# Side work of a block's mixers ordered behind the main work on VectorE, and one mixer's norm moved a round later

## The chip, the cores and the metric

The kernel runs on one core of a Trainium2 chip. The metric is the device time of one execution in microseconds (us); three executions of the kernel before were timed, and a further one was profiled.

## What is computed

Two transformer layers (attention and a convolutional MLP, 1024 tokens of width 1024) are followed by one block with four parallel mixers. The change lies in that last block alone. Cut to what matters:

```
proj = h @ w_in                         # 11 slots of 512 columns
(va, za, bb, bc, bv, zb, ca, cg, zc, dv, zd) = split(proj, 11)
ya = rglru(va)                          # a: two-way gated linear scan
yb = bb * depthwise_conv(bc * bv, 3)    # b
u = ca * sigmoid(cg)                    # c: 31-tap depthwise convolution,
u = depthwise_conv(u, c_conv, 15, 15)   #    layer norm over the 512 channels,
u = layer_norm(u, c_ln_g, c_ln_b)       #    silu, 512 x 512 matmul
yc = silu(u) @ c_pw + c_pw_b
yd = (pool_grid(dv) @ d_w + d_b) * d_scale   # d: box means of four sizes
cat = [ya * silu(za), yb * silu(zb), yc * silu(zc), yd * silu(zd)]
x = x + gate * (cat @ w_out);  return rms_norm(x)
```

## The kernel before

Tokens lie along the free axis (1024, as two halves of 512), channels on the 128 partitions. Every fp32 matmul is three fp32r matmuls of high and low pieces (`mm3`): the high piece is cast on ScalarE (ACT, L239), the low one subtracted on GpSimd or VectorE (POOL or DVE, L240). A projected "slot" (one of the 11 column groups, one of four 128-channel chunks c) is 48 matmuls of 128x512 into a two-bank PSUM tile with tag A, of which there are two.

The last block (`block2`) runs four rounds, c = 0 to 3, one 128-channel chunk of every mixer in each. A round emits: `a_conv` (slot 0, copied to SBUF by ACT on L1474, then six taps on DVE, L1327), `d_pool` (slot 9, copied on L1474; two scans on DVE, L1621 and L1625, with windows and products on POOL between and behind them), `mixer_b` (slots 3, 4, 2, 5: products on DVE on L1568 and L1573, a gate on L1493), `a_gates`, `d_end`, then `a_back` (ACT's exponentials after a switch to the table set LNEXP, DVE's products and scans on L1351 to L1354, POOL's sum on L1601), the gate of slot 1, the product for the concatenation (`cat`, L1498), and `out_proj`: the output projection of the chunks that are done, added up by DVE on L1522.

Mixer c is spread over the rounds. `mixer_c(k)` forms the gated input of chunk k (L1557) and puts 30 taps of its convolution (L1549) into a queue of side work, `bg`; each tap is a DVE pass over 1024 tokens. `tick()`, called some twenty times a round, emits the next 2 (from the end of round 0 on, 3) steps of that queue into the program. When the convolutions are through, the queue goes on with `c_var`: per half, mean over the channels (L1647 and L1649 on DVE, a matmul with ones on L1651), subtraction (L1662), squares, mean again. The rest of the norm is `c_norm` (ACT L1675, L1676; three small DVE passes L1677 to L1679; four products L1682, two on DVE and two on POOL, per half), then `c_silu` (ACT L1692, L1693; DVE L1694; the split), and at the end `c_end`, the 512 x 512 matmul with its DVE pass on L1708.

In the kernel before, `bg.drain()` and `c_norm` stand in round 2, `c_norm` behind `a_back`; `c_silu` stands in round 3, ahead of the switch to LNEXP. What comes behind the rounds is `c_end` for both halves, `out_proj` of a's last chunk, and per half the output projection of mixer c and `finish` (scaling, residual, RMS norm; its reciprocal root is Ln and Exp on ACT, L254 and L255).

The emitted order is not the order on the engines: the framework runs a scheduler that lays out each engine's instructions by its own timing model, under the data dependencies and under ordering hints that the kernel adds. A DVE tap of the side queue that is emitted behind a main instruction may so be laid ahead of it. Buffers come from rings: `p` has 5 buffers, `cb` 3, `q` 10.

Of the kernel before, what the change touches and what calls it, by code (L numbers as in the profile page):

```python
# [61 lines left out]
LNEXP, SIG, GELU = "natural_log_exp_and_others", "sigmoid_and_others", "gelu_apprx_tanh_and_others"  # L62
# [33 lines left out]
class Net:  # L96
# [146 lines left out]
    def halves(self, tag):  # L243

        while True:
            t = self.t(tag)
            for k in range(0, BUFS[tag][0], 512):
                yield t[:, k:k + 512]
# [1191 lines left out]
    def block2(self, xs, src):  # L1440
        nc, I = self.nc, self.I
# [2 lines left out]

        rate = [BGN]

        def tick():
            for _ in range(rate[0]):
                bg.step()

        def slots_first():

            load = lambda ss: [self.weight(I["wi2"][s * 4]) for s in ss]
            a = [self.ps("A") for _ in range(2)]
            b = [[], []]
            for n, w in enumerate(load((7, 6))):
                self.proj(w, xs, 0, a[n][:, 0:512])
            ws = load((3, 4))
            for hf, tags in enumerate(("OT", "JT")):
                for n in range(2):  # L1460
                    b[n].append(self.ps(tags[n]))
                    self.proj(ws[n], xs, hf, b[n][hf])
            for n, w in enumerate(load((7, 6))):
                self.proj(w, xs, 1, a[n][:, 512:1024])
            return {(7, 0): a[0], (6, 0): a[1], (3, 0): b[0], (4, 0): b[1]}
# [85 lines left out]
        def mixer_c(c):  # L1551
            pg = slot(7, c)
            t = self.t("q")
            nc.scalar.activation(t, pg, AF.Sigmoid)
            tick()
            pa = slot(6, c)
            nc.vector.tensor_tensor(out=t, in0=pa, in1=t, op=ALU.mult)  # L1557
            y = self.t("v")
            bg.add(conv(y, t, [self.pcol("c_conv", k * 4 + c) for k in range(31)], 15))
            tick()  # L1560
            return y

        def mixer_b(c):
            t = copied("p", slot(3, c))
            tick()
            pv = slot(4, c)
            for o, i in zip(halves(t), pv) if isinstance(pv, list) else ((t, pv),):
                nc.vector.tensor_tensor(out=o, in0=i, in1=o, op=ALU.mult)  # L1568
            tick()
            y = self.t("p")  # L1570
            run(conv(y, t, [self.pcol("b_conv", k * 4 + c) for k in range(3)], 1))
            pb = slot(2, c)
            nc.vector.tensor_tensor(out=y, in0=pb, in1=y, op=ALU.mult)  # L1573
            tick()
            return cat(y, gated(5, c))

        def a_conv(c):
            v = copied("p", slot(0, c))
            tick()
            xs_ = []  # L1580
            for d in range(2):
                xc, xh, xl = self.t("q"), self.t("q", F32R), self.t("q", F32R)
                self.rg_conv(v, T, c, d, xc, (xh, xl))
                xs_.append((xc, (xh, xl)))
            return xs_

        def a_gates(c, xs_):
            gates = self.weight(I["wrg"][c], 512)
            units = []
            for d, (xc, xhl) in enumerate(xs_):  # L1590
                r, th = self.t("q"), self.t("q")
                self.rg_gates(T, c, d, gates, xc, r, th, xhl, self.t("p"))
                units.append((c, d, xc, r, th))
                tick()
            return units
# [18 lines left out]
        def d_pool(c):  # L1614
            ps = slot(9, c)
            u, P, S, mask = copied("p", ps), *(self.t("p") for _ in range(3))
            h = 2 ** c
            ones = lambda n, v: nc.gpsimd.memset(mask.rearrange("p (r q) -> p r q", q=n)[:, :, 0:1], v)
            nc.gpsimd.memset(mask, 1.0)
            ones(64, 0.0)  # L1620
            nc.vector.tensor_tensor_scan(out=P, data0=mask, data1=u, initial=0.0, op0=ALU.mult, op1=ALU.add)  # L1621
            tick()
            window(S.rearrange("p (q r) -> p r q", r=16), P.rearrange("p (r q) -> p r q", q=64), h)
            ones(16, 0.0)
            nc.vector.tensor_tensor_scan(out=P, data0=mask, data1=S, initial=0.0, op0=ALU.mult, op1=ALU.add)  # L1625
            window(S.rearrange("p (r q) -> p q r", q=64), P.rearrange("p (q r) -> p q r", r=16), h)
            rc = self.t("p")
            nc.sync.dma_start(rc, I["rcnt"][c])
            nc.gpsimd.tensor_tensor(out=S, in0=S, in1=rc, op=ALU.mult)
            nc.gpsimd.tensor_tensor(out=S, in0=S, in1=u, op=ALU.subtract)  # L1630
            h, l = self.t("q", F32R), self.t("q", F32R)
            self.split(S, h, l, nc.gpsimd)
            return h, l

        def d_end(c, hl):
            z = gated(10, c)
            wd = self.weight(I["dw"], 512)
            y = self.t("p")
            for hf in range(2):
                ps = self.psM()  # L1640
                self.mm3(ps, [(tuple(p[:, c * 128:c * 128 + 128] for p in wd), tuple(halves(p)[hf] for p in hl))])
                nc.scalar.activation(halves(y)[hf], ps, AF.Identity, scale=self.pcol("d_scale", c), bias=self.dbs[:, c:c + 1])
            return cat(y, z)
# [28 lines left out]
        def c_norm(u, vs):  # L1672
            for hf, var in enumerate(vs):
                a, b = halves(self.t("p"))
                nc.scalar.activation(a, var, AF.Ln, bias=self.lneps, scale=1.0)  # L1675
                nc.scalar.activation(b, a, AF.Exp, scale=-0.5)  # L1676
                nc.vector.scalar_tensor_tensor(out=a, in0=var, scalar=LN_EPS, in1=b, op0=ALU.add, op1=ALU.mult)  # L1677
                nc.vector.scalar_tensor_tensor(out=a, in0=a, scalar=-0.5, in1=b, op0=ALU.mult, op1=ALU.mult)
                nc.vector.scalar_tensor_tensor(out=b, in0=a, scalar=1.5, in1=b, op0=ALU.add, op1=ALU.mult)  # L1679
                for c, p in enumerate(u):  # L1680
                    x = halves(p)[hf]
                    (nc.gpsimd if c % 2 else nc.vector).tensor_tensor(out=x, in0=x, in1=b, op=ALU.mult)  # L1682

        def c_silu(u, hf):

            out = []
            for c, p in enumerate(u):
                t = halves(p)[hf]
                g, bb = self.pcol("ln_g", c), self.pcol("ln_b", c)
                h, l = self.t("x", F32R), self.t("x", F32R)  # L1690
                q = self.t("cb")[:, 0:512]
                nc.scalar.activation(q, t, AF.Sigmoid, scale=g, bias=bb)  # L1692
                nc.scalar.activation(t, t, AF.Identity, scale=g, bias=bb)  # L1693
                nc.vector.tensor_tensor(out=t, in0=t, in1=q, op=ALU.mult)  # L1694
                self.split(t, h, l, nc.gpsimd if c % 2 else nc.vector)
                out.append((h, l))
            return out
# [18 lines left out]
        us, vs = [mixer_c(0)], []  # L1716
# [3 lines left out]
        for c in range(4):  # L1720
            if c:
                ax = a_conv(c)
                dx = d_pool(c)
                catb = mixer_b(c)
            units = a_gates(c, ax)
            catd = d_end(c, dx)
            if c == 3:
                za = gated(1, c)
                z = [gated(8, k) for k in range(4)]
                s = [c_silu(us, hf) for hf in range(2)]  # L1730
            if c == 2:
                bg.drain()
            self.act_set(LNEXP)
            ya = a_back(units)
            if c == 2:
                c_norm(us, vs)
            if c < 3:
                self.act_set(SIG)
                za = gated(1, c)
                for k in ((1, 2), (3,), ())[c]:  # L1740
                    us.append(mixer_c(k))
                    if k == 3:
                        bg.add(c_var(us, vs))
                rate[0] = 3
            if c < 2:
                out_proj([(1, c, catb), (3, c, catd), (0, c, cat(ya, za))], first=c == 0)
            else:
                out_proj([(1, c, catb), (3, c, catd)])
                cata = cat(ya, za)
                if c == 2:  # L1750
                    out_proj([(0, c, cata)])
# [215 lines left out]
```

## Time and profile before

| | |
|---|---|
| time, median of 3 runs | 3844.7 us (3842.88 to 3845.17) |
| profiled execution: time, span | 3847.31 us, 3845.5 us |
| TensorE (PE) busy | 3491.9 us, 91% |
| VectorE, ScalarE, GpSimd busy | 2513.1, 1831.1, 1991.7 us |
| mean granted TensorE clock | 0.969 of full speed |

The span is the time from the first to the last instruction in the profile; the profiled execution's own time is 1.8 us longer and 2.6 us over the median. The last block takes roughly the last 780 us of the span.

### The profile page before, as it was taken

How to read it: one execution, taken by the hardware profiler on the slowest of the kernel's cores; microseconds unless marked ns; L12 is line 12 of the kernel's file. 1: busy time of each engine (PE TensorE's matmuls, PEld its weight loads, DVE VectorE, ACT ScalarE, POOL GpSimd, SP SyncE). 2: the span in 40 equal slices, each digit the busy share in tenths (PEclk: the TensorE clock that was granted, in tenths of full speed). 3: DMA queues.
4: the chain of work that ended last, by engine and by line, in shares of the span. 5: the costliest groups of instructions: out<-in, count | busy, mean ns of one | idle time of the engine just before them, and what ended most of it. 6: DMA issues, size and time to landing. Idle time of an engine off the chain costs nothing. (4 is left out here: it accounts for less than half of the span.)

```text
span 3845.5 us, 47528 instructions
## 1 busy us (share of the span) xinstructions
PE 3491.9 (91%) x16588; PEld 2827.6 (74%) x16588; DVE 2513.1 (65%) x3432; ACT 1831.1 (48%) x3300; POOL 1991.7 (52%) x1480
## 2 busy tenths in 40 slices
PE   6999899889999999999889889999988979898998
PEld 4788678667777777778678767887766768686776
DVE  5566865888888551567885776665545288685547
ACT  4455755444445343355664454545575333324333
POOL 3445433636667564534533546666655454545544
PEclk9999999899999999999999899999989989999999
DMA  3643553432323552454473432222634211111114
GB/s 100 163 119 127 193 170 129 134 123 100 110 88 128 189 173 73 112 135 140 140 231 122 133 116 90 73 82 88 191 120 141 68 45 52 44 50 38 56 50 145
DMA packets 217473, 440.12 MB, mean 114 GB/s; under 512 B 28432, under 2 KB 52240, under 8 KB 217232
## 3 DMA queue, kind: packets, MB, share of 16 engines
q1 hardware_dynamic: 217232, 437.08, 35.5%
q8 instruction: 130, 2.13, 0.2%
q14 instruction: 111, 0.91, 0.1%
HBM read 313.75 MB, written 104.34 MB: 109 GB/s over the span
## 5 line engine op out<-in xcount | busy, mean ns | idle before, releaser
L233 PE MATMUL AZ<-xZ,whZ 128*128 128x512 f32 x2880 | 907.4, 396 | 51.5 <-ACT pZ L1474 14.4
L240 POOL TENSOR_TENSOR wlZ<-wrZ,whZ 128x512 fp32r<-128x512 f32 x340 | 488.7, 1452 | 553.9 <-ACT whZ L239 474.9
L233 PEld LDWEIGHTS AZ<-xZ,whZ 128*128 128x128 f32 x2880 | 545.4, 191 | 178.9 <-issue 20.0
L233 PE MATMUL AZ<-xZ,wlZ 128*128 128x512 f32 x1440 | 567.1, 396 | 10.9 <-POOL wlZ L240 10.7
L524 POOL TENSOR_TENSOR ptZ<-pfZ,ptZ 128x512 fp32r<-128x512 f32 (+1 forms) x200 | 264.2, 1321 | 363.7 <-DVE ptZ L523 337.7
L233 PE MATMUL JZ<-xZ,whZ 128*128 128x512 f32 (+1 forms) x1248 | 403.7, 401 | 41.3 <-ACT whZ L239 21.6
L239 ACT CAST whZ<-wrZ 128x512 fp32r<-128x512 f32 x340 | 196.9, 608 | 431.7 <-issue 141.2
L240 POOL TENSOR_TENSOR wlZ<-qZ,whZ 128x512 fp32r<-128x512 f32 x200 | 279.5, 1413 | 202.7 <-ACT whZ L239 202.7
L233 PEld LDWEIGHTS AZ<-xZ,wlZ 128*128 128x128 f32 x1440 | 275.0, 191 | 74.4 <-POOL wlZ L240 16.8
L522 ACT COPY pfZ<-TZ 128x512 f32<-128x512 f32 (+2 forms) x400 | 220.6, 556 | 211.6 <-PE TZ L517 130.6
L233 PEld LDWEIGHTS JZ<-xZ,whZ 128*128 128x128 f32 (+1 forms) x1248 | 223.1, 186 | 101.0 <-ACT whZ L239 31.5
L540 PE MATMUL OZ<-ptZ,vZ 128*128 128x256 f32 (+1 forms) x1344 | 262.3, 307 | 33.2 <-POOL ptZ L524 12.5
L523 DVE CAST ptZ<-pfZ 128x512 fp32r<-128x512 f32 (+2 forms) x400 | 220.0, 552 | 107.1 <-ACT pfZ L522 91.9
L517 PE MATMUL TZ<-ident,pZ 128*128 128x128 f32 x1488 | 243.7, 284 | 21.6 <-ACT pfZ L522 12.3
L240 POOL TENSOR_TENSOR wlZ<-vZ,whZ 128x512 fp32r<-128x512 f32 x144 | 181.8, 1283 | 149.3 <-ACT whZ L239 149.0
L540 PEld LDWEIGHTS OZ<-ptZ,vZ 128*128 128x128 f32 x1344 | 205.2, 197 | 58.8 <-POOL ptZ L524 16.6
L233 PE MATMUL JZ<-xZ,wlZ 128*128 128x512 f32 (+1 forms) x624 | 245.9, 394 | 0.0
L233 PE MATMUL TZ<-xZ,whZ 128*128 128x512 f32 x736 | 230.2, 394 | 2.6 <-DVE pZ L256 1.5
L517 PEld LDWEIGHTS TZ<-ident,pZ 128*128 128x128 f32 x1488 | 182.0, 145 | 53.6 <-ACT pfZ L522 21.3
L233 PE MATMUL AZ<-qZ,whZ 128*128 128x512 f32 x592 | 191.7, 406 | 31.7 <-ACT pjZ L1157 23.0
L562 DVE TENSOR_REDUCE s1Z<-AZ 128x1 f32<-128x1024 f32 x128 | 156.0, 1221 | 67.1 <-PE AZ L233 35.8
L1549 DVE SCALAR_TENSOR_TENSOR vZ<-qZ,pv,vZ 128x1009 f32<-128x1009 f32 (+14 forms) x120 | 194.8, 1642 | 4.1 <-ACT vZ L1539 2.4
(515 smaller groups left out, 7942.5 us busy)
## 6 DMA issues: line engine op xcount, KB each, us to landing
qZ<-wup SPq DMA_DIRECT2D x80, 512.0 KB, 3.3
wrZ<-wi SPq DMA_DIRECT2D x156, 256.0 KB, 2.7
vZ<-wdn SPq DMA_DIRECT2D x48, 512.0 KB, 3.6
sc_g<-vZ SPq DMA_DIRECT2D x44, 512.0 KB, 3.6
qZ<-sc_pr SPq DMA_DIRECT2D x40, 512.0 KB, 4.9
wrZ<-wo SPq DMA_DIRECT2D x64, 256.0 KB, 2.8
sc_ot<-cbZ SPq DMA_DIRECT2D x56, 256.0 KB, 2.5
xZ<-sc_ot SPq DMA_DIRECT2D x56, 256.0 KB, 5.5
```

Of the source, the lines that this page charges most:

```text
L233: self.nc.tensor.matmul(ps, lhsT=a, rhs=b, start=first and k == 0, stop=last and k == n - 1, skip_group_check=parts)
L239: nc.scalar.copy(h, full)
L240: (eng or nc.vector).tensor_tensor(out=l, in0=full, in1=h.bitcast(F32), op=ALU.subtract)
L517: nc.tensor.transpose(ps[:, n:n + 128], blk, self.ident)
L522: nc.scalar.copy(pf[:, 0:n], ps[:, 0:n])
L523: nc.vector.tensor_copy(ph[:, 0:n], pf[:, 0:n])
L524: (nc.gpsimd if SHARE[self.turn2 % len(SHARE)] else nc.vector).tensor_tensor(out=pl[:, 0:n], in0=pf[:, 0:n], in1=ph[:, 0:n].bitcast(F32), ...
L540: nc.tensor.matmul(o[:, c0:c0 + w], lhsT=v, rhs=x[:, at[k]:at[k] + w], start=(k == order[0] and x is ph), stop=(k == order[-1] and x is pl ...
L562: nc.vector.tensor_reduce(out=nmx, in_=ps, axis=AX.X, op=ALU.max, negate=True)
L1549: nc.vector.scalar_tensor_tensor(out=o, in0=i, scalar=w[k], in1=o, op0=ALU.mult, op1=ALU.add)
```

## The change

It does two things. First, `tick()` now looks at the program emitted since its last call, notes the last DVE instruction of the main work, and gives every DVE instruction of the side steps that it emits a hint to be scheduled behind that one (an order without a semaphore). Second, `bg.drain()` and `c_norm` go from round 2 to round 3; there `c_norm` follows `a_back`, and `c_silu` follows `c_norm` behind one more switch of the table set, back to SIG.

```
+        seen = [0, None]
+        later = mybir.DependencyInfo(mybir.DependencyClass.NoSync, mybir.DependencyReason.SCHED_ONLY)
         def tick():
+            ins = list(nc.cur_bb.bb.instructions)
+            for i in ins[seen[0]:]:
+                if i.engine == mybir.EngineType.DVE:
+                    seen[1] = i.name
+            n = len(ins)
             for _ in range(rate[0]):
                 bg.step()
+            ins = list(nc.cur_bb.bb.instructions)
+            for i in ins[n:]:
+                if seen[1] and i.engine == mybir.EngineType.DVE:
+                    self.tc.add_manual_dep(i, seen[1], later, reason="side")
+            seen[0] = len(ins)
...
             if c == 3:
                 za = gated(1, c)
                 z = [gated(8, k) for k in range(4)]
-                s = [c_silu(us, hf) for hf in range(2)]
-            if c == 2:
                 bg.drain()
             self.act_set(LNEXP)
             ya = a_back(units)
-            if c == 2:
+            if c == 3:
                 c_norm(us, vs)
+                self.act_set(SIG)
+                s = [c_silu(us, hf) for hf in range(2)]
```

The line numbers of the changed kernel are 14 higher inside the block (L1549 becomes L1563, L1573 becomes L1587, L1498 becomes L1512). The order of the instructions on the engines moves as follows.

VectorE, round 0, mixer b. Before: its first products (L1568), its two taps (on tile pZ_27790), the product with slot 2 (L1573) and the gate of slot 5 (L1493); vZ_27614 is the side convolution of chunk 0.

```order
L1568 TENSOR_TENSOR pZ_27781<-TZ_27518,pZ_27781 128x512
L1549 SCALAR_TENSOR_TENSOR vZ_27614<-qZ_27611,pv,vZ_27614 128x1020
L1549 SCALAR_TENSOR_TENSOR vZ_27614<-qZ_27611,pv,vZ_27614 128x1019
L1549 SCALAR_TENSOR_TENSOR pZ_27790<-pZ_27781,pv,pZ_27790 128x1023
L1549 SCALAR_TENSOR_TENSOR vZ_27614<-qZ_27611,pv,vZ_27614 128x1018
L1549 SCALAR_TENSOR_TENSOR pZ_27790<-pZ_27781,pv,pZ_27790 128x1023
L1549 SCALAR_TENSOR_TENSOR vZ_27614<-qZ_27611,pv,vZ_27614 128x1017
L1573 TENSOR_TENSOR pZ_27790<-AZ_27804,pZ_27790 128x1024
```

The same place in the changed kernel:

```order
L1582 TENSOR_TENSOR pZ_27781<-TZ_27518,pZ_27781 128x512
L1563 SCALAR_TENSOR_TENSOR vZ_27614<-qZ_27611,pv,vZ_27614 128x1016
L1563 SCALAR_TENSOR_TENSOR vZ_27614<-qZ_27611,pv,vZ_27614 128x1017
L1563 SCALAR_TENSOR_TENSOR pZ_27790<-pZ_27781,pv,pZ_27790 128x1023 x2
L1587 TENSOR_TENSOR pZ_27790<-AZ_27804,pZ_27790 128x1024
L1563 SCALAR_TENSOR_TENSOR vZ_27614<-qZ_27611,pv,vZ_27614 128x1018
L1563 SCALAR_TENSOR_TENSOR vZ_27614<-qZ_27611,pv,vZ_27614 128x1019
L1507 TENSOR_TENSOR pZ_27915<-AZ_27866,pZ_27915 128x1024
```

From the start of the round to the product with slot 2, 22 side taps stand on VectorE before and 9 in the changed kernel; the other 13 have moved behind it.

VectorE, round 1, mixer a's six taps (tiles qZ_28720 and qZ_28729) and the first scan of mixer d (L1635). In the changed kernel they stand in a row:

```order
L1563 SCALAR_TENSOR_TENSOR vZ_27614<-qZ_27611,pv,vZ_27614 128x1009
L1327 SCALAR_TENSOR_TENSOR qZ_28720<-pZ_28715,pv,qZ_28720 128x1023
L1327 SCALAR_TENSOR_TENSOR qZ_28720<-pZ_28715,pv,qZ_28720 128x1022
L1327 SCALAR_TENSOR_TENSOR qZ_28720<-pZ_28715,pv,qZ_28720 128x1021
L1327 SCALAR_TENSOR_TENSOR qZ_28729<-pZ_28715,pv,qZ_28729 128x1023
L1327 SCALAR_TENSOR_TENSOR qZ_28729<-pZ_28715,pv,qZ_28729 128x1022
L1327 SCALAR_TENSOR_TENSOR qZ_28729<-pZ_28715,pv,qZ_28729 128x1021
L1635 SCALAR_TENSOR_TENSOR pZ_28799<-pZ_28801,pZ_28797 128x1024
```

Before, the end of a run of 35 side taps stands ahead of them, and further ones between them:

```order
L1647 TENSOR_TENSOR cbZ_30269<-vZ_27614,vZ_28273 128x512
L1549 SCALAR_TENSOR_TENSOR vZ_28399<-qZ_28335,pv,vZ_28399 128x1023
...
L1549 SCALAR_TENSOR_TENSOR vZ_28399<-qZ_28335,pv,vZ_28399 128x1020
L1327 SCALAR_TENSOR_TENSOR qZ_28720<-pZ_28715,pv,qZ_28720 128x1023
L1549 SCALAR_TENSOR_TENSOR vZ_28399<-qZ_28335,pv,vZ_28399 128x1019
L1327 SCALAR_TENSOR_TENSOR qZ_28720<-pZ_28715,pv,qZ_28720 128x1022
```

VectorE, round 3, behind the last additions of the output projection (L1536, L1522 before). In the changed kernel:

```order
L1536 TENSOR_TENSOR pfZ_28651<-JZ_31766,pfZ_28651 128x512
L1512 TENSOR_TENSOR pZ_31268<-qZ_30717,pZ_31268 128x1024
L1691 SCALAR_TENSOR_TENSOR pZ_31533<-cbZ_30401,pZ_31533 128x512
L1692 SCALAR_TENSOR_TENSOR pZ_31533<-pZ_31533 128x512
L1693 SCALAR_TENSOR_TENSOR pZ_31533<-pZ_31533 128x512
L1696 TENSOR_TENSOR vZ_27614<-vZ_27614,pZ_31533 128x512
L1696 TENSOR_TENSOR vZ_28399<-vZ_28399,pZ_31533 128x512
L1691 SCALAR_TENSOR_TENSOR pZ_31543<-cbZ_30462,pZ_31543 128x512
...
L1696 TENSOR_TENSOR vZ_28399<-vZ_28399,pZ_31543 128x512
L1708 TENSOR_TENSOR vZ_27614<-vZ_27614,cbZ_31556 128x512
L1708 TENSOR_TENSOR vZ_28273<-vZ_28273,cbZ_31564 128x512
```

Before, `c_end` (L1708) follows the product for the concatenation at once:

```order
L1522 TENSOR_TENSOR pfZ_28651<-JZ_31765,pfZ_28651 128x512
L1498 TENSOR_TENSOR pZ_31288<-qZ_30737,pZ_31288 128x1024
L1708 SCALAR_TENSOR_TENSOR pZ_31350<-TZ_31788,pv,pZ_31350 128x512
L240 TENSOR_TENSOR xZ_31803<-pZ_31350,xZ_31802 128x512
L1708 SCALAR_TENSOR_TENSOR pZ_31412<-OZ_31806,pv,pZ_31412 128x512
```

So the whole norm and activation of mixer c now stand between the last main product and `c_end`. On TensorE, `out_proj` of a's last chunk stands behind `c_end` in both kernels. On ScalarE the set left at the end is SIG, and four ACT_TABLE_LOADs have appeared in `finish`, one ahead of each Ln (L254) and one ahead of each Exp (L255).

## Rows read from the trace of the kernel before

**Rows 1.** The page, part 1: busy time, share, instructions.

```profile
PE 3491.9 (91%) x16588; PEld 2827.6 (74%) x16588; DVE 2513.1 (65%) x3432; ACT 1831.1 (48%) x3300; POOL 1991.7 (52%) x1480
```

**Rows 2.** Waits of TensorE in the last block: total us, times, longest.

```profile
PE AZ L233 <- ACT pZ L1474: 14.4, 3, 11.5
PE AZ L233 <- DVE pZ L1573: 13.6, 1, 13.6
PE JZ L233 <- DVE ptZ L1522: 8.2, 3, 6.6
PE AZ L233 <- POOL wlZ L240: 4.8, 3, 2.5
PE OZ L233 <- DVE ptZ L1522: 4.2, 2, 3.3
...
PE TZ L233 <- DVE pjZ L1522: 3.0, 1, 3.0
PE AZ L233 <- DVE pZ L1493: 2.6, 1, 2.6
```

**Rows 3.** Windows of rounds 0 and 1: us, busy per engine, then clock, DMA.

```profile
3110.00:3150.00 40.00, 22.28 (x88) 17.63 (x87) 39.97 (x21) 8.51 (x13) 30.87 (x12) 0.81 0.12 39
...
3290.00:3320.00 30.00, 16.52 (x62) 12.92 (x63) 29.93 (x16) 5.83 (x10) 20.48 (x13) 0.83 0.16 52
```

**Rows 4.** Timeline of VectorE, round 0: start, us, instructions, [idle before].

```profile
3085.55 13.92 DVE L1549 SCALAR_TENSOR_TENSOR vZ<-qZ,pv,vZ 128x1009 f32<-128x1009 f32 x9 [1.22 <-ACT vZ L1539]
...
3113.17 2.28 DVE L1621 TENSOR_TENSOR_SCAN pZ<-pZ,pZ 128x1024 f32<-128x1024 f32 x1
...
3136.54 3.35 DVE L1549 SCALAR_TENSOR_TENSOR pZ<-pZ,pv,pZ 128x1023 f32<-128x1023 f32 x1
...
3147.49 1.21 DVE L1573 TENSOR_TENSOR pZ<-AZ,pZ 128x1024 f32<-128x1024 f32 x1
```

**Rows 5.** Timeline of ScalarE, round 0: the copy of slot 9.

```profile
3106.61 1.00 ACT L1474 COPY pZ<-AZ 128x1024 f32<-128x1024 f32 x1
```

**Rows 6.** Timeline of GpSimd, round 0.

```profile
3124.08 2.74 POOL L1609 TENSOR_TENSOR pZ<-pZ 128x896 f32<-128x896 f32 x1 [5.55 <-DVE pZ L1625]
...
3138.78 4.44 POOL L240 TENSOR_TENSOR wlZ<-wrZ,whZ 128x512 fp32r<-128x512 f32 x2
```

**Rows 7.** Timeline of VectorE, round 1.

```profile
3228.87 46.31 DVE L1549 SCALAR_TENSOR_TENSOR vZ<-qZ,pv,vZ 128x1023 f32<-128x1023 f32 x31
...
3299.50 2.27 DVE L1621 TENSOR_TENSOR_SCAN pZ<-pZ,pZ 128x1024 f32<-128x1024 f32 x1
```

**Rows 8.** Chain that ended last, round 3: start, us, work.

```profile
3667.24 54.25 PE AZ L233 x238
```

**Rows 9.** Timeline of ScalarE, round 3.

```profile
3722.91 1.28 ACT L175 ACT_TABLE_LOAD   x1
3724.20 1.16 ACT L1348 ACTIVATE qZ<-qZ,spm8Z 128x1024 f32<-128x1024 f32 x1
```

**Rows 10.** Timeline of GpSimd, round 3: the low piece of za's product.

```profile
3750.77 2.40 POOL L240 TENSOR_TENSOR qZ<-pZ,qZ 128x1024 fp32r<-128x1024 f32 x1
```

**Rows 11.** Timeline of VectorE, first and last of eight passes of c_end.

```profile
3749.52 0.74 DVE L1708 SCALAR_TENSOR_TENSOR pZ<-TZ,pv,pZ 128x512 f32<-128x512 f32 x1
...
3767.57 0.75 DVE L1708 SCALAR_TENSOR_TENSOR pZ<-JZ,pv,pZ 128x512 f32<-128x512 f32 x1 [0.36 <-PE JZ L233]
```

**Rows 12.** Groups by form, 3535 to 3570: busy us, mean ns, idle before.

```profile
L1682 POOL TENSOR_TENSOR vZ<-vZ,pZ 128x512 f32<-128x512 f32 x4 | 7.1, 1784 | 9.3 <-DVE pZ L1679 9.3
...
L1682 DVE TENSOR_TENSOR vZ<-vZ,pZ 128x512 f32<-128x512 f32 x4 | 5.9, 1508 | 0.0
...
L1692 ACT ACTIVATE cbZ<-vZ,pv 128x512 f32<-128x512 f32 x6 | 4.8, 812 | 5.2 <-DVE vZ L1694 5.2
...
L1675 ACT ACTIVATE pZ<-cbZ,lneps 128x512 f32<-128x512 f32 x2 | 1.4, 716 | 0.0
...
L1678 DVE SCALAR_TENSOR_TENSOR pZ<-pZ 128x512 f32<-128x512 f32 x2 | 1.4, 678 | 0.0
```

## The prediction

> **What bounds the kernel now.** I read the page first: TensorE is busy 91% of the span [rows 1], so time can be won only where it stands still or runs at a low clock, and lost where it is made to. Next the waits of TensorE in the last block, the only part touched [rows 2]. The reader is to see three kinds. In rounds 0 and 1 TensorE waits for PSUM banks that mixer b or d hold: 13.6 us for one product on VectorE, 11.5 us for one copy on ScalarE, and smaller ones (2.6 us for a gate). Three waits are for low weight pieces from GpSimd, 4.8 us together. And 15.4 us (8.2 + 4.2 + 3.0) are waits for the additions of the output projection, nearly all of them in round 2. The windows come third: in the two big gaps VectorE is busy all the time (39.97 of 40 us, 29.93 of 30), TensorE little over half, and its granted clock is 0.81 and 0.83, a mean over stretches at 2.4 and at 1.2 GHz [rows 3]. So behind each gap the first matmuls run at half rate for some us more. The timelines, read last, say what VectorE did meanwhile: side taps of mixer c stood in front of the work that TensorE wanted [rows 4, 7].
>
> **Round 0.** The order shows 13 of 22 side taps moved behind the product with slot 2. Nine taps took 13.92 us, 1.55 each [rows 4], so VectorE itself could reach that product 13 x 1.55 = 20 us sooner. The inputs allow less. The first scan, at 3113.17, needs the copy that ended at 3107.6 [rows 4, 5], so it and all behind it can come at most 5.5 us sooner. Behind the second scan stands GpSimd's chain, which begins with the window at 3124.08 and ends with the low weight pieces at 3138.78 + 4.44 = 3143.2 [rows 6], 19.1 us. These are the weights of the next slot, wanted right after the product. With the scans 5.5 to 6 us sooner they are there at about 3137. The product itself: window, copies, its first products, four taps of 1.3 to 3.35 us [rows 4] bring it to about 3132, 15 us sooner. So GpSimd's pieces become what is late next. TensorE resumes near 3137 instead of 3148.8: 11.8 us, and some 2 us of the half-clock stretch behind the gap. I take 13 us. Ends: 5 us if GpSimd's chain doesn't move (3143.2), 17 us if only the product counts.
>
> **Rounds 1 and 2.** Before, 31 side taps take 46.31 us and hold up mixer a's taps and with them the first scan, at 3299.50 [rows 7]. The copy for which TensorE waits 11.5 us needs a `p` buffer that the second scan's window frees. In the changed order a's six taps stand in a row, with six side taps fewer up to the second scan and four fewer just ahead. At 1.5 (46.31 / 31) to 2.8 us each that is 15 to 28 us; I take 16, since other engines then join. That is more than 11.5, so this wait goes whole, as do the other two copy waits (14.4 - 11.5 = 2.9), two of the three GpSimd waits (4.8 - 2.5 = 2.3), and about 3.7 us of lost clock: 20.4 us. Given back: GpSimd forms mixer d's low piece ahead of weights in the new order, one 1024-wide pass of 2.4 us [rows 10] or more, I take 3; mixer d's gates come 17 matmuls later, 17 x 0.228 = 3.9 us (0.228 is 54.25 / 238 [rows 8]), in which their weights wait; the product for the concatenation comes some 1 us later in round 1, and a second low piece 2 us in round 2. Of the 2.6 us for L1493 about 1 goes. Sum 20.4 - 3 - 3.9 - 1 - 2 + 1 = 11.5, taken as 12; ends 4 (everything is given back twice) and 20.
>
> **Round 2.** Out go the norm and the activation: two products of 1.51 us per half [rows 12] stood between additions of the output projection, and with them the waits of 3.3 and 3.0 us [rows 2]. In comes the first half of `c_var`, which before ran ahead of this stretch: three additions and four subtractions of 0.7 us and the wait for the squares, about 8 us in the same queue. Five side taps that are now later come here too; I put them into VectorE's waits. 6.3 against 8, taken as a loss of 1.5 us; ends a gain of 4 and a loss of 6.
>
> **Round 3.** TensorE's last slot ends at 3667.24 + 54.25 = 3721.5 [rows 8]. Left ahead of `c_end` is the projection of two chunks, 96 matmuls or 21.9 us, with small waits to about 3744. Before, `c_end` starts then, because mixer c's tiles have been ready since round 2, under matmuls that cover them. That cover is gone. `c_norm` needs a buffer of the ring `p`, and its five hold four gates z, in use until `c_end`, and za, free when GpSimd has its low piece, at 3750.77 + 2.40 = 3753.2 [rows 10]. From there, by [rows 12]: Ln and Exp 2 x 0.72, three passes 3 x 0.68, four products (GpSimd's two, 2 x 1.78): 3760.2. The second half must take the same buffer, so its Ln waits for all four products: 1.4, then the table load of 1.28 us [rows 9] to 3762.9. Its passes and products end near 3767, and on VectorE they stand ahead of the first half's activation, so the first tile of `c_end` is ready near 3768 and the fourth some 8 us later, one each 2 us (Sigmoid 0.81, Identity, product, split). `c_end` ran over 18.8 us from its first pass to its last (3749.52 to 3768.3 [rows 11]). Starting 23 to 24 us late, thinned out at first and at half clock, it ends near 3793. Loss 25 us; ends 20 (no thinning, products uncontended) and 28.
>
> **The tail.** The set left is SIG, so both halves of `finish` load tables for Ln and Exp. The load ahead of Ln lies in idle time; that ahead of Exp is on the path. One load is 1.28 us, and the next activation starts right behind it (3722.91 + 1.28, then 3724.20 [rows 9]). Two loads: 2.6, of which the first half's is partly hidden; loss 2 us, ends 1 and 3. The Trainium skill, ScalarE: Activation LUTs, section What ACT_TABLE_LOAD costs, has another price, about 2.66 us for a switch, with a drain of 1.38 us beside the load. The row shows no such drain; by the Trainium skill the sum would be some 4 us worse, three switches being on the path.
>
> **The sum.** 13 + 12 - 1.5 - 25 - 2 = 3.5 us lost, on 3847.3 us: 3850.8. The profiled execution is 2.6 us over the median of the runs shown, so the time to expect is 3848.2, taken as 3848. About 0.2%, 7.7 us, is what a measurement of this kernel can tell from no change, so the band without a change is 3837 to 3852.4.
>
> **The rivals.** *Faster.* VectorE was the only cause of the waits in rounds 0 to 2, and nothing is given back. Then round 0 wins 17 and rounds 1 and 2 win 20, and round 2's waits for additions end 2 us better: 39 - 25 - 2 = 12 won, 3847.3 - 12 - 2.6 = 3833. For it: VectorE is full in both windows while ScalarE is busy 8.5 and 5.8 us. Against: GpSimd is busy 30.87 of 40 us [rows 3] and has its own order. It decides if the low weight pieces of round 0 are ready by 3133. Chance 0.19.
>
> *Slower, through round 2.* The side work held back in rounds 0 and 1 has still to run, and it piles up where `c_var` must end: each tap beside a GpSimd pass costs up to 3.35 us [rows 4], each mean makes TensorE wait for VectorE, and the additions of the output projection stand behind them. If its 15.4 us of waits grow by two thirds, 10 us, the time is 3858. For it: the waits of [rows 2] sit here already, and banks T, O and J hold only four additions. Against: before, the same stretch carried the norm too. It decides if over five taps are left for the projection of round 2. Chance 0.33.
>
> *Slower, through the switches.* A switch of the table set holds ScalarE for twice its row; three on the path cost 3 x 1.28 = 3.8 us more: 3852, and with any small loss over the band. The same rule of the Trainium skill, in the same section, speaks for it. The trace speaks against it. Chance 0.05.
>
> That the hints change nothing is no rival: 9 taps against 22.
>
> **How the numbers follow.** My forecast, a time within 0.2%, has 0.43; faster 0.19; slower 0.33 + 0.05 = 0.38. The bounds of the terms (about 6, 8, 5, 4 and 1 us to either side) add in squares to 12 us; widened to 14, so that it takes in most of the rivals on either side, the range is 3834 to 3862.
>
> **What would show it.** Right: L1587 near 3132 and TensorE resuming near 3137; in round 1 no copy wait over 3 us; in round 3 TensorE idle for some 23 us behind about 3744 minus what was won, at half clock after, and released by tiles of L1708 or its splits; four table loads in `finish`. Wrong: round 3's idle time under 15 us, because the norm finds another buffer; a new wait over 8 us in rounds 0 to 2; or an output projection of round 2 that takes more than 6 us longer than before.

## The result: slower by 0.7%

The changed kernel takes 3873.1 us (median of 3 runs, 3869.3 to 3873.2) against 3844.7 us: ratio 1.0073, interval 1.0059 to 1.0088. The forecast was 3848 us, no change, with a range up to 3862; the time lies above it. The profiled execution took 3873.23 us, its span is 3871.5 us.

The waits of TensorE in the last block, changed kernel (total us, times, longest), answer to [rows 2]:

```profile
PE TZ L233 <- ACT xZ L239: 22.9, 1, 22.9
PE AZ L233 <- POOL wlZ L240: 10.3, 5, 2.9
PE AZ L233 <- DVE pZ L1587: 8.9, 1, 8.9
PE OZ L233 <- DVE ptZ L1536: 5.8, 2, 4.9
PE TZ L1665 <- DVE cbZ L1663: 5.2, 2, 3.8
PE TZ L233 <- POOL qZ L240: 4.9, 1, 4.9
PE TZ L233 <- POOL wlZ L240: 3.2, 4, 1.3
PE TZ L233 <- ACT qZ L1340: 2.8, 1, 2.8
```

The copy wait of 11.5 us is gone, and the 13.6 us for the product of round 0 are 8.9. In their place stand one wait of 22.9 us ahead of `c_end`, twice the waits for GpSimd's low pieces, and new ones: for mixer a's gates (L1340), for a low piece of 4.9 us and for the means of `c_var` (L1663).

To see where the time went I cut the block at the same places in every trace: the first matmul on an A tile (slot 7 of round 0), the last of the 16 copies of round 0's projection (L1520, L1534 in the changed kernel), the 16th and the 48th addition of the projections on VectorE (ends of rounds 1 and 2), the last matmul on an A tile (end of round 3's slots), and the end of the span. Each cut is the start of that row in the timeline; the columns are differences in us. The first row is the kernel before, the second the changed one; the rest are the experiments below, all from one profiled execution each.

| | round 0 | round 1 | round 2 | slots of 3 | to the end | ratio of times |
|---|---|---|---|---|---|---|
| before | 185.7 | 168.0 | 158.5 | 136.9 | 124.4 | 1 |
| changed | 175.7 | 169.7 | 166.2 | 136.9 | 153.9 | 1.0073 |
| e1_order_only | 175.7 | 168.2 | 174.1 | 136.9 | 124.4 | 1.0014 |
| e2_move_only | 186.0 | 168.0 | 153.5 | 136.9 | 153.1 | 1.0057 |
| e3_set_back | 175.7 | 169.3 | 165.7 | 136.9 | 151.9 | 1.0063 |
| e4_free_input_early | 175.7 | 157.8 | 165.9 | 136.9 | 152.3 | 1.0046 |
| e5_norm_other_ring | 175.7 | 169.8 | 166.2 | 136.9 | 149.5 | 1.0056 |
| e7_cover | 175.6 | 169.3 | 165.7 | 136.9 | 152.8 | 1.0079 |
| e8_order_round0 | 175.7 | 174.8 | 160.2 | 137.1 | 124.4 | 0.9998 |
| e9_norm_top_round3 | 185.6 | 167.9 | 163.2 | 134.2 | 124.7 | 1.0011 |
| e10_rate4 | 175.7 | 171.3 | 157.6 | 136.9 | 153.0 | 1.0055 |
| e11_norm_behind | 185.7 | 167.9 | 153.6 | 139.5 | 124.5 | 0.9986 |
| e12_all | 175.6 | 171.3 | 157.7 | 139.5 | 124.5 | 0.9989 |
| e13_rate4_before | 186.0 | 168.1 | 159.7 | 136.9 | 124.4 | 1.0005 |

So the changed kernel wins 10.0 us in round 0, loses 1.7 and 7.7 in rounds 1 and 2, and 29.5 behind the last slot: 28.9 lost from the first cut to the end. (The spans differ by 26.0, because the stretch ahead of the first cut, which the change doesn't touch, was 2.9 us shorter in this execution; over the traces here it ends between 3064.7 and 3077.3 us.) Between kernels that share the edit, rounds 0 and 2 and the slots of round 3 repeat to within 0.6 us, round 1 and the end to within 1.6 us; so the 1.7 us of round 1 are hardly more than scatter. That is still far better than whole times: 27 runs of the kernel before in one of the comparisons below took 3839 to 3850 us, and 23 in another 3836 to 3853.

The windows of rounds 1 and 2 (us, then busy time of PE, PEld, DVE, ACT and POOL, granted TensorE clock, DMA), first before, then changed:

```profile
3257.68:3425.67 167.99, 151.18 (x654) 123.39 (x653) 123.27 (x86) 51.09 (x71) 85.26 (x46) 0.97 0.15 47
3425.67:3584.18 158.51, 139.01 (x567) 108.67 (x566) 117.31 (x111) 66.49 (x93) 78.91 (x46) 0.96 0.13 41
```

```profile
3244.75:3414.45 169.70, 155.77 (x652) 125.22 (x651) 129.16 (x85) 50.46 (x70) 91.92 (x46) 0.96 0.15 47
3414.45:3580.66 166.21, 143.13 (x569) 110.80 (x568) 142.54 (x113) 53.38 (x74) 79.97 (x42) 0.93 0.12 39
```

Over the two rounds TensorE stands still 36.3 us before (168.0 less 151.2 and 158.5 less 139.0) and 37.0 us after. So the copy waits that went were replaced, to within 1 us, by others, and nearly all of the 9.4 us lost is TensorE taking longer over the same matmuls, 298.9 us busy for 290.2, at a granted clock that fell from 0.97 to 0.96 and from 0.96 to 0.93.

Round 1. Timelines of ScalarE, VectorE and TensorE of the changed kernel, in that order; in brackets the idle time before a row and who ended it:

```profile
3322.66 0.68 ACT L1340 ACTIVATE pZ<-OZ,pv 128x512 f32<-128x512 f32 x1
3330.93 0.69 ACT L1340 ACTIVATE qZ<-TZ,pv 128x512 f32<-128x512 f32 x1 [7.59 <-DVE vZ L1563]
...
3335.21 1.14 ACT L239 CAST whZ<-wrZ 128x512 fp32r<-128x512 f32 x2
```

```profile
3318.25 3.42 DVE L1512 TENSOR_TENSOR pZ<-pZ,pZ 128x1024 f32<-128x1024 f32 x1
3321.59 11.80 DVE L1563 SCALAR_TENSOR_TENSOR vZ<-qZ,pv,vZ 128x1009 f32<-128x1009 f32 x8
```

```profile
3331.67 0.50 PE L233 MATMUL TZ<-qZ,whZ 128*128 128x512 f32 x1 [2.79 <-ACT qZ L1340]
...
3339.11 0.79 PE L233 MATMUL AZ<-xZ,wlZ 128*128 128x512 f32 x1 [2.50 <-POOL wlZ L240]
```

ScalarE stands 7.6 us at a gate of mixer a, and what ends the wait is a side tap on VectorE. The gate's Sigmoid reads PSUM, not the convolution; what it shares with the tap is memory. Its result r goes into a buffer of the ring `q` that held the input of chunk 1's side convolution, and that input is read until the last of its taps. Held back by the hints, the last tap ends at 3330.9, and so does the wait. Behind the gate the casts of weights wait, behind them GpSimd's low pieces.

Round 3, ScalarE, TensorE and VectorE of the changed kernel:

```profile
3749.53 0.72 ACT L1689 ACTIVATE pZ<-cbZ,lneps 128x512 f32<-128x512 f32 x1 [2.45 <-POOL qZ L240]
3750.28 0.63 ACT L1690 ACTIVATE pZ<-pZ 128x512 f32<-128x512 f32 x1
3756.70 0.72 ACT L1689 ACTIVATE pZ<-cbZ,lneps 128x512 f32<-128x512 f32 x1 [5.79 <-POOL vZ L1696]
...
3758.10 1.28 ACT L175 ACT_TABLE_LOAD   x1
3759.40 2.22 ACT L1706 ACTIVATE cbZ<-vZ,pv 128x512 f32<-128x512 f32 x3
...
3764.43 0.62 ACT L239 CAST xZ<-vZ 128x512 fp32r<-128x512 f32 x1 [0.69 <-DVE vZ L1708]
```

```profile
3765.10 0.79 PE L233 MATMUL TZ<-xZ,whZ 128*128 128x512 f32 x1 [22.87 <-ACT xZ L239]
```

```profile
3790.51 0.75 DVE L1722 SCALAR_TENSOR_TENSOR pZ<-JZ,pv,pZ 128x512 f32<-128x512 f32 x1 [0.15 <-PE JZ L233]
```

The first Ln starts when GpSimd's low piece has freed za, the second when the last product has freed the same buffer, as the prediction had it. Counted from the last slot, which comes 3.5 us earlier in this trace, both starts are within 0.2 us of the predicted times. `c_end` ends 73.7 us after the last slot (3791.3 less 3717.6) against 47.2 before (3768.3 less 3721.1): 26.5 lost. From there to the end it is 80.2 against 77.2. The last Ln and Exp on ScalarE, before:

```profile
3833.37 0.69 ACT L254 ACTIVATE vZ<-JZ,eps 128x512 f32<-128x512 f32 x1 [3.32 <-PE JZ L278]
3834.09 0.63 ACT L255 ACTIVATE vZ<-vZ 128x512 f32<-128x512 f32 x1
```

In the changed kernel, with the table loads:

```profile
3855.64 1.28 ACT L254 ACT_TABLE_LOAD   x1 [3.31 <-PE JZ L278]
3856.93 0.69 ACT L254 ACTIVATE vZ<-JZ,eps 128x512 f32<-128x512 f32 x1
3857.64 1.28 ACT L255 ACT_TABLE_LOAD   x1
3858.93 0.63 ACT L255 ACTIVATE vZ<-vZ 128x512 f32<-128x512 f32 x1
```

The load ahead of Ln carries the wait for TensorE's sum: it doesn't run in the idle time ahead of it. So both loads of the last half are on the path, 2.6 us. Where the same four loads stand in other traces (e2, e4, e5 and e10 below) the stretch from `c_end` to the end takes 79.2 us, 2.0 more than before. The rest in this trace, about 1.1 us, lies behind the last Exp (11.9 us to the end of the span in place of 10.8); it also shows in e7 and, without any loads, in e3, and its cause isn't known.

### The profile page after: what moved, and what is told of

Same layout as the page of the kernel before. It is cut to its first block, busy times and chain, and to the rows that moved or that the text cites. A ratio compares the mean times of both kernels' runs of the same rounds, so it can differ in the third digit from the quotient of the medians.

```text
span 3871.5 us, 47534 instructions
## 1 busy us (share of the span) xinstructions
PE 3505.2 (91%) x16588; PEld 2836.5 (73%) x16588; DVE 2530.0 (65%) x3432; ACT 1836.4 (47%) x3305; POOL 2001.8 (52%) x1480
## 5 line engine op out<-in xcount | busy, mean ns | idle before, releaser
L240 POOL TENSOR_TENSOR wlZ<-wrZ,whZ 128x512 fp32r<-128x512 f32 x340 | 501.0, 1489 | 568.9 <-ACT whZ L239 486.8
L233 PEld LDWEIGHTS AZ<-xZ,whZ 128*128 128x128 f32 x2880 | 549.7, 192 | 157.5 <-issue 14.6
L240 POOL TENSOR_TENSOR wlZ<-vZ,whZ 128x512 fp32r<-128x512 f32 x144 | 180.7, 1276 | 151.2 <-ACT whZ L239 151.0
L233 PE MATMUL TZ<-xZ,whZ 128*128 128x512 f32 x736 | 232.8, 396 | 25.4 <-ACT xZ L239 22.9
L1563 DVE SCALAR_TENSOR_TENSOR vZ<-qZ,pv,vZ 128x1022 f32<-128x1022 f32 (+14 forms) x120 | 222.8, 1869 | 3.0 <-ACT vZ L1553 1.2
```

Of the source, the lines that this page charges most:

```text
L233: self.nc.tensor.matmul(ps, lhsT=a, rhs=b, start=first and k == 0, stop=last and k == n - 1, skip_group_check=parts)
L240: (eng or nc.vector).tensor_tensor(out=l, in0=full, in1=h.bitcast(F32), op=ALU.subtract)
L1563: nc.vector.scalar_tensor_tensor(out=o, in0=i, scalar=w[k], in1=o, op0=ALU.mult, op1=ALU.add)
```

## The experiments

Theory A: the move of the norm is what costs, the hints win a little. Theory B: the hints cost. All ratios are to the kernel before on the same chip.

**e1_order_only** is the kernel before with the new `tick()` alone, **e2_move_only** the changed kernel with the old one.

> Only the ordering hints of tick(); drain, norm and activation of mixer c stay in round 2 as before. Theory A (the loss of the change is the norm of mixer c without cover in round 3 and the table loads behind it, about 29 us; the hints themselves are worth a few us): 3836 to 3846 us, no wait over 3 us ahead of c_end, four table loads of finish gone; if the hints pile side work up in round 2 together with the norm, the upper end. Theory B (the hints are what costs): 3855 us or more.

Measured: 1.0014 (1.0004 to 1.0024), 3852.8 against 3848.1 us, above the 3836 to 3846 expected of A and below the 3855 of B. The end is as before (124.4), so the loss there is not the hints'. But they win nothing over the block: 10.0 us in round 0, and 15.6 lost in round 2. Its longest waits:

```profile
PE TZ L1665 <- DVE cbZ L1663: 12.1, 1, 12.1
PE AZ L233 <- POOL wlZ L240: 10.8, 5, 3.0
PE AZ L233 <- DVE pZ L1587: 8.9, 1, 8.9
PE JZ L1665 <- DVE cbZ L1663: 8.1, 1, 8.1
```

TensorE waits 20 us for the sums of `c_var`, which need the last of the side taps that were held back and, on VectorE, stand behind them and behind mixer a's scans.

> Only the move of drain, norm and activation to round 3; no hints, side taps as before. Theory A: about 23 us of idle TensorE ahead of c_end here too, the same gaps of 13.6 and 11.5 us in rounds 0 and 1 as before, some 3 to 6 us less waiting in round 2 because the norm is out: 3864 to 3872 us. Theory B: at most 3855 us.

Measured: 1.0057 (1.0045 to 1.0070), 3869.0 us, as A had it: 28.7 us lost at the end, 5.0 won in round 2, rounds 0 and 1 as before. The two parts nearly add up: 4.6 us by the medians for the hints and 20.9 for the move are 25.5, and the whole change costs 28.4.

**e4_free_input_early**: 8 of 31 taps of one chunk read another tile, so values differ.

```diff
-                nc.vector.scalar_tensor_tensor(out=o, in0=i, scalar=w[k], in1=o, op0=ALU.mult, op1=ALU.add)
+                nc.vector.scalar_tensor_tensor(out=o, in0=o if k >= own else i, scalar=w[k], in1=o, op0=ALU.mult, op1=ALU.add)
...
-            bg.add(conv(y, t, [self.pcol("c_conv", k * 4 + c) for k in range(31)], 15))
+            bg.add(conv(y, t, [self.pcol("c_conv", k * 4 + c) for k in range(31)], 15, 23 if c == 1 else 99))
```

> The changed kernel, but the last 8 taps of chunk 1's convolution read the accumulator in place of the input tile (same instructions and order, other values), so that the input's q buffer comes free 8 taps earlier. Theory A (part on round 1: mixer a's gate tile takes that buffer, so ScalarE and behind it a weight cast and its low piece wait for the last side tap): the waits of 2.8, 0.8 and 2.5 us near the gates of round 1 shrink to under 2 us together, with them 2 us of half clock; 3864 to 3868 us. Rival (GpSimd shared with more taps sets these waits): the same waits stay, 3873 us.

Measured: 1.0046 (1.0034 to 1.0058), 3864.1 us. Round 1 takes 157.8 us, 11.9 less than in the changed kernel and 10.2 less than before, the rest as in the changed kernel to within 1.6 us. Its window of round 1:

```profile
3253.00:3410.76 157.76, 150.21 (x652) 122.88 (x651) 132.41 (x84) 50.58 (x70) 93.17 (x46) 0.99 0.15 50
```

The wait for L1340 is gone; those for the low pieces near it, which the rival put down to the shared engines, have shrunk (2.50 to 1.45 us for the longest). More came back than the 6 to 8 us expected: two later waits (2.1 and 2.3 us) went too. Of the 11.9 us, 6.4 are TensorE standing still less (13.9 to 7.6 us) and 5.6 are less busy time, at a clock of 0.99 in place of 0.96. The order did not quite stay, as the expectation had it: with the buffer free, the scheduler laid mixer a's Sigmoids closer together on ScalarE, and on VectorE the product for the concatenation and the first additions ahead of a side tap or two. So 11.9 us is the price of the held buffer together with the order that follows from it.

**e10_rate4** gets the buffer free with nothing left out, by more steps a tick; **e13_rate4_before** is its control without the hints.

```diff
-                rate[0] = 3
+                rate[0] = 4
```

> The changed kernel, but tick() emits 4 side steps in place of 3 from the end of round 0 on, so that chunk 1's convolution ends ahead of mixer b's product in round 1 and its input's q buffer is free before mixer a's gates want it; nothing is left out. Theory (the held buffer is what the hints cost in round 1, and with the shared engines nothing else of that size): first slot to last slot of the rounds 636 to 641 us in the trace, against 648.5 of the changed kernel and 649.2 of before; from there to the end 152 to 154 us as in the changed kernel; ratio to before 1.004 to 1.006. Rival (taps ahead of the main work are the cost, so more of them earlier is worse): rounds 648 us or more, ratio 1.0073 or more.

Measured: 1.0055 (1.0042 to 1.0068). The rounds take 641.5 us, 7.0 less than in the changed kernel, 0.5 over the range. Mixer a's gate no longer waits, but round 1 is no shorter (171.3 us): a wait of 6.0 us for a gate's product on VectorE (L1507) has come, so freeing the buffer this way did not win what e4_free_input_early won. What is won is round 2, 157.6 us in place of 166.2.

```profile
PE TZ L1665 <- DVE cbZ L1663: 12.3, 1, 12.3
PE AZ L233 <- DVE pZ L1507: 6.4, 2, 6.0
```

> The kernel before with 4 side steps per tick from the end of round 0 on and nothing else. It tells whether the step count by itself does what e10_rate4 shows. Theory (without the hints the scheduler lays the taps ahead of the main work anyway): the waits of 13.6 and 11.5 us stay within 2 us, rounds 647 to 655 us, ratio 0.999 to 1.002. Rival (the count does it): rounds under 643 us.

Measured: 1.0005 (0.9997 to 1.0014), with the waits of 13.6 and 11.5 us unchanged: the step count alone does nothing.

```profile
PE AZ L233 <- DVE pZ L1573: 13.6, 1, 13.6
PE AZ L233 <- ACT pZ L1474: 13.1, 2, 11.5
```

**e8_order_round0** lets the hints act in round 0 only.

```diff
-                if seen[1] and i.engine == mybir.EngineType.DVE:
+                if seen[1] and rate[0] == BGN and i.engine == mybir.EngineType.DVE:
```

> The kernel before with the ordering hints in round 0 only (while two steps are emitted per tick); norm and activation where they were. Theory (the hints win some 10 us in round 0 and lose in rounds 1 and 2, where the held-back taps meet the gates, the weights and c_var): ratio to before 0.9965 to 0.9985. Rival (the taps pushed out of round 0 cost the same in round 1): 1.000 to 1.0015.

Measured: 0.9998 (0.9988 to 1.0008), between the two. Round 0 wins its 10.0 us, round 1 loses 6.8 of them (the copy wait grows from 11.5 to 14.6 us, and one of 3.5 us follows it), round 2 another 1.7. Here the work pushed out of one round is paid in the next.

**e5_norm_other_ring** and **e7_cover** ask what sets the 22.9 us ahead of `c_end`.

```diff
-                a, b = halves(self.t("p"))
+                a, b = halves(self.t("q"))
```

> The changed kernel, but the norm of mixer c takes its tiles from the ring q instead of p, so that it need not wait for za nor the second half for the first. Theory A (the chain starts when za's buffer comes free): Ln and Exp move up under the output projection, the idle stretch ahead of c_end falls from 22.9 to 9 to 13 us, time 3859 to 3864 us. Rival (the place behind the last product on VectorE sets it, buffers or not): idle falls by no more than 4 us, 3869 to 3873 us.

Measured: 1.0056 (1.0044 to 1.0068), 3867.7 us; the idle stretch is 20.2 us. The rival held for the wait, 2.7 us less; the time came out a little under its 3869. The first Ln starts at 3733.65, some 15 us earlier, yet the rest of the norm runs between additions and scans of VectorE and ends little sooner:

```profile
3747.95 1.21 DVE L1512 TENSOR_TENSOR pZ<-qZ,pZ 128x1024 f32<-128x1024 f32 x1
3749.09 1.28 DVE L1693 SCALAR_TENSOR_TENSOR qZ<-qZ 128x512 f32<-128x512 f32 x2
3750.29 7.85 DVE L1696 TENSOR_TENSOR vZ<-vZ,qZ 128x512 f32<-128x512 f32 x4
3758.06 2.95 DVE L1708 TENSOR_TENSOR vZ<-vZ,cbZ 128x512 f32<-128x512 f32 x3
```

The four products take 7.85 us beside GpSimd's, and the product for the concatenation comes at 3747.95 in place of 3743.74 (5.2 us later, counted from the last slot), since small passes of the norm now stand ahead of it.

e7_cover emits `out_proj([(0, 3, cata)])` ahead of the two `c_end` calls.

> The changed kernel, but the output projection of a's last chunk, 48 matmuls or 10.9 us, is emitted ahead of c_end in place of behind it. Theory A (the loss of round 3 is uncovered time of TensorE): this work fills half of the 22.9 us, the rest stays idle in two pieces of 7 and some 5 us; some 3 us come back behind c_end, whose splits lose their cover. Ratio to before 1.0045 to 1.006. Rival (VectorE is what the chain waits for, and the 16 additions of this projection stand ahead of the norm): the first tile of c_end comes as much later as the projection takes, ratio 1.007 to 1.008.

Measured: 1.0079 (1.0066 to 1.0093). The rival held again. TensorE's long wait falls apart into shorter ones (4.4, 1.1, 1.2, 4.8 and 5.5 us), but the end is only 1.1 us nearer the last slot, which is within the scatter: the 16 additions of the projection lie between the norm's passes on VectorE, and the splits behind `c_end` have lost their cover. So it was not matmuls alone that were missing there.

**e3_set_back** adds `self.act_set(LNEXP)` behind the activation.

> The changed kernel with one more switch of the table set, back to LNEXP behind the activation of mixer c, so that finish needs no loads of its own. Theory (two of the four loads are on the path, 1.28 us each): from the last pass of c_end to the end of the span 77 to 78 us in place of 80.2; 0.993 to 1.000 of the changed kernel's 1.0073 over before, that is 1.006 to 1.0073. Rival (each switch costs 2.7 us): that stretch 75 us.

Measured: 1.0063 (1.0046 to 1.0080). From the last pass of `c_end` (3787.5) to the end (3865.8) it is 78.3 us, 1.9 less than 80.2, a little outside the 77 to 78. The 1.1 us behind the last Exp, described above, are in both; without them it is the 77.2 of before. The four loads cost 1.9 us, no more than two of their 1.28 us, less than the rival said.

**e9_norm_top_round3** and **e11_norm_behind** look for a better place: the top of round 3, ahead of the slots.

```diff
+            if c == 3:
+                bg.drain()
+                main = [i.name for i in nc.cur_bb.bb.instructions if i.engine == mybir.EngineType.DVE][-1]
+                n = len(nc.cur_bb.bb.instructions)
+                self.act_set(LNEXP)
+                c_norm(us, vs)
+                for i in list(nc.cur_bb.bb.instructions)[n:]:
+                    if i.engine == mybir.EngineType.DVE:
+                        self.tc.add_manual_dep(i, main, mybir.DependencyInfo(
+                            mybir.DependencyClass.NoSync, mybir.DependencyReason.SCHED_ONLY), reason="norm")
+                self.act_set(SIG)
```

e9 is this without the lines on `main`, `n` and the loop; both take drain and norm out of round 2.

> The kernel before, no hints; drain and norm of mixer c at the top of round 3, behind the output projection of round 2 and ahead of 120 us of slots that cover it; activation ahead of a_back as before. Theory A (what the move costs is the missing cover, what it wins is the norm out of round 2's projection): no idle stretch ahead of c_end, 4 to 7 us fewer waits in round 2, ratio to before 0.998 to 0.9995. Rival (the norm gets laid into round 2's projection by the scheduler again): 1.000.

Measured: 1.0011 (1.0000 to 1.0021), the rival: emitted behind the projection, the norm was still laid into it (L1522 are additions, L1677 and L1682 the norm), and round 2 takes 163.2 us, 4.7 more than before.

```profile
3559.90 0.69 DVE L1522 TENSOR_TENSOR pjZ<-TZ,pjZ 128x512 f32<-128x512 f32 x1
3560.50 3.07 DVE L1682 TENSOR_TENSOR vZ<-vZ,pZ 128x512 f32<-128x512 f32 x2
3563.49 0.68 DVE L1677 SCALAR_TENSOR_TENSOR pZ<-cbZ,pZ 128x512 f32<-128x512 f32 x1
3564.09 0.68 DVE L1522 TENSOR_TENSOR ptZ<-OZ,ptZ 128x512 f32<-128x512 f32 x1
```

> The kernel before, no hints in tick(); drain and norm at the top of round 3 with a hint that lays the norm's VectorE work behind the last addition of round 2's output projection; activation ahead of a_back as before. Theory (the move wins some 5 us in round 2 and its whole cost is the place behind a_back): rounds 643 to 646 us, from the last slot to the end 124 to 125 us, ratio to before 0.998 to 0.9995. Rival (the norm costs as much under the slots of round 3, by GpSimd and ScalarE, as in round 2): rounds 648 to 651 us, ratio 1.000 to 1.001.

Measured: 0.9986 (0.9977 to 0.9995), 3838.0 against 3844.3 us, the fastest version here, though not clear of e12_all below. Round 2 wins 4.9 us, as in e2_move_only, the end stays at 124.5, and the slots of round 3 give 2.6 back. From the first cut to the end that is 2.3 us, 0.06%; the rest of the 0.14% isn't seen in the traces, and the interval allows for either. The norm now starts behind the last addition:

```profile
3571.95 0.69 DVE L1522 TENSOR_TENSOR pfZ<-OZ,pfZ 128x512 f32<-128x512 f32 x1
3572.56 3.44 DVE L1677 SCALAR_TENSOR_TENSOR pZ<-cbZ,pZ 128x512 f32<-128x512 f32 x2
```

**e12_all** joins e10's hints and rate with e11's place.

> The hints of tick(), 4 steps per tick from the end of round 0 on, and the norm placed as in e11_norm_behind. Theory: the gains add up: rounds 632 to 641 us, last slot to the end 124 to 125 us, ratio to before 0.995 to 0.998. Rival (side work held back meets the norm in round 2 as in e1_order_only): rounds 648 us or more, ratio 1.000 or more.

Measured: 0.9989 (0.9981 to 0.9998): faster than before, no faster than e11_norm_behind. The rounds take 644.1 us, above the 632 to 641 expected. Round 0 wins 10.1, round 1 loses 3.3, round 2 wins 0.8; the hints' gain is again spent where the taps come to lie.

## Why the prediction was wrong, by its own steps

**Round 0** was right in kind and 3 us too large: 10.0 for 13. The changed trace:

```profile
3133.88 1.23 DVE L1587 TENSOR_TENSOR pZ<-AZ,pZ 128x1024 f32<-128x1024 f32 x1
```

The first cut comes 2.9 us earlier here than in the trace before, so on the prediction's clock TensorE resumes at 3138.1 (3135.25 here; predicted near 3137) and this product starts at 3136.8, 4.8 us later than the 3132 predicted. The product was the last to come, not GpSimd's pieces, which were ready at 3136.1 in this trace and wanted a little later. So the resume time came out nearly right in part by luck. The four taps ahead of the product took 11.9 us beside GpSimd, 3.0 each, near the upper end of what was allowed. TensorE resumed 10.7 us sooner, for the 11.8 predicted, and of the 2 us of half clock that were to come on top none did: up to the end of the round 0.7 us were lost again.

**Rounds 1 and 2** are the step that failed: 12 us won were predicted, with 1.5 lost in round 2's projection, and 9.4 were lost. The part that was foreseen came: the copy waits are gone. Two terms were wrong. The term "given back", 9.9 us, was put together from order and engines alone, and waits of the same size as those won came in place of them (36.3 us of standing still before, 37.0 after). It left out that a side tap that is held back holds its input: with that input free, and the order that follows from it, round 1 takes 11.9 us less (e4_free_input_early); freed by more steps a tick it won nothing in round 1 (e10_rate4). And the 3.7 us of lost clock that were to be won back turned into a loss: TensorE was busy 8.7 us longer over the two rounds. The clock that was not granted, as a share of each window, comes to about 11 us before (0.03 of 168.0 and 0.04 of 158.5) and about 18 after (0.04 of 169.7 and 0.07 of 166.2), so as an estimate up to 7 of the 8.7 are the clock.

The side work held back also arrives in round 2, which was the rival "slower, through round 2": the hints cost 12.7 us there with the norm gone (166.2 less 153.5) and 15.6 with it. The rival's reason fits e1_order_only, where the means of `c_var` take 20 us. In the changed kernel the waits at the means (5.2 and 1.5 us) are shorter than in e2_move_only without the hints (9.4 us). What it has more than e2_move_only in this round is one wait of 4.9 us for a low piece on GpSimd, behind a product for the concatenation (L1512), one of 4.9 us for an addition, and 4.0 us for low pieces of weights (1.4 there). Eleven side taps ran on VectorE between 3491 and 3513, ahead of that product, and four more between 3523 and 3537, around the first additions; the rival had asked for over five there. The product, the low piece and TensorE behind it:

```profile
3513.43 1.22 DVE L1512 TENSOR_TENSOR pZ<-pZ,pZ 128x1024 f32<-128x1024 f32 x1
```

```profile
3521.53 3.32 POOL L240 TENSOR_TENSOR qZ<-pZ,qZ 128x1024 fp32r<-128x1024 f32 x1
```

```profile
3524.90 0.80 PE L233 MATMUL TZ<-qZ,whZ 128*128 128x512 f32 x1 [4.94 <-POOL qZ L240]
```

The move by itself wins 5.0 in round 2, so its norm was priced about right.

**Round 3**, 25 us predicted, measured 26.5, with an idle stretch of 22.9 us for the 23 to 24 predicted. The size is right, and so, counted from the last slot, are the times of Ln and of the first tile. The reason was half right: 48 matmuls put into the gap brought the end nearer by no more than the scatter (e7_cover), and za's buffer is only 3.4 us of it (e5_norm_other_ring: 70.3 us from the last slot to the end of `c_end` in place of 73.7). What is left is the length of the chain on VectorE and ScalarE, and its place among VectorE's additions, once it starts behind `a_back`. Started ahead of the slots it costs 2.6 us (e11_norm_behind).

**The tail**, 2 us predicted, measured 3.0, of which setting the table set back recovers 1.9; the other 1.1 us are not of the loads, and in four more traces with the loads the tail costs 2.0, as predicted. The reason was half right: the load ahead of the last Ln was on the path too. The Trainium skill, ScalarE: Activation LUTs, section What ACT_TABLE_LOAD costs, gives 2.66 us a switch; here the next activation starts 1.29 us after the load began (3857.64, 3858.93), so the trace doesn't agree.

By the steps, 10.0 won and 9.4, 26.5 and 3.0 lost make 28.9 us lost, where 3.5 were predicted; 22.9 of the difference of 25.4 are rounds 1 and 2 (12 - 1.5 against -9.4 is 19.9) and round 0 (3.0), the rest round 3 and the tail (2.5).

What stays open: which of the taps costs what in round 2; the path through L1512 is read from the timelines and no run isolates it. e10_rate4 shows that the loss goes when they end earlier (157.6 us), but there a wait of 12.3 us for `c_var` has moved up between the slots, so it isn't one wait that was removed. None of the prediction's own signs of being wrong showed: round 3's idle time was not under 15 us, no new wait in rounds 0 to 2 was over 4.9 us, and from its first addition to its last the projection of round 2 took 51.4 us for 48.9. Signs set for one large wait do not see many small ones and a lower clock.

## What to carry to other kernels

Work that is held back can hold its inputs: before side work is ordered later, ask in which ring its input lies and what wants that buffer next. A gain read from one wait has to be followed to where the displaced work goes; here the later rounds paid for what round 0 gained. Waits that vanish are not yet time won: add up all of them, and the clock, over the whole stretch. And a chain moved behind the last main work stood on the path here, 22.9 us, and the matmuls put beside it did not cover it; the same chain, ordered behind one projection and ahead of the slots, was worth 0.14% (0.05 to 0.23).

## What was not expected of the hardware

A table load can wait with the activation that it serves: the load at 3855.64 started only when TensorE's sum was there, after 3.31 us of idle ScalarE. In the first half the load ran at 3829.84, ahead of its activation's wait, and was hidden.
